# Raw weights and the conditioning matrix in 2 KB pieces through two rings, column sums and value weights a step apart, unread products at the norms

## The chip, the cores and the metric

The kernel runs on one core of a Trainium2 chip. The metric is the device time of one execution in microseconds (us); the kernel is built with Tile, a layer that puts every instruction into its engine's queue by a priority (the order of the program text, unless it is shifted) and adds the semaphores. The engines are TensorE (PE, with its weight loads PEld), VectorE (DVE), ScalarE (ACT), GpSimd (POOL) and SyncE (SP), which here does nothing but issue transfers. Each engine takes its own queue in order.

## The reference

One decoder layer on 512 tokens of width 2048, all in float32. Cut to what matters:

```
mod = silu(c) @ w_mod + b_mod                  # conditioning matrix: 2048 x 12288
sh1, sc1, g1, sh2, sc2, g2 = split(mod, 6)
h = rms_norm(x, norm_attn) * (1 + sc1) + sh1
qa, ka, va, qb, ckv, qi, ki, wi = split(h @ w_in)
out_a = sliding_window_attention(qa, ka, va, sinks, bias)     # 16 heads, window 128
out_b = sparse_attention(qb, rms_norm(ckv), w_uk, w_uv,       # 16 heads, 128 keys a query,
                         qi, ki, wi, bias)                    # chosen by the indexer's scores
x = x + g1 * (concat(out_a, out_b) @ w_out)
h = rms_norm(x, norm_ffn) * (1 + sc2) + sh2
u, g = split(h @ w_up)                                        # 2 x 5632 columns
x = x + g2 * ((silu(causal_conv3(u)) * g) @ w_down)
return rms_norm(x, norm_final)
```

## The kernel before

**Products.** Activations lie with their features on the partitions. A float32 product is made of three matmuls: weights and activations are each split into a rounded part and the rest (ACT casts, DVE subtracts), and `mm3` adds high by high, high by low and low by high.

**Slots.** The work of the big products is a list of *slots*. One slot is a quarter of a unit (128 output columns): 512 columns of raw weights, four `mm3`, so twelve matmuls. `drive` (L305) walks through the list. For slot i it asks for the raw weights up to `AHEAD_LOAD` slots ahead, for their split up to `AHEAD_SPLIT` = 3 slots ahead, gives PE the slot's matmuls, and then takes one `step()`: every running generator is advanced to its next `yield`. These generators are the rest of the work: the attention of a pair of heads (`pair_gen`), the keys and values of the next pair (`prep_gen`, L810), the convolution, and, last in each step, the conditioning matrix (`mod_gen`, L203).

**Raw weights.** `load_raw` (L120) loads one whole unit, 1 MB with 8 KB in each partition, into the ring `raw` of three buffers. Its four slots split their quarters from it (L128, L129), and the buffer comes free after the last. The same ring holds the indexer's weights (`fetch_qi`) and, in the attention stage and early in the gated MLP, the conditioning matrix (`ring_mod`).

**The conditioning matrix** is 24 groups of 512 columns, each of 16 row tiles. A group's row tiles come as four 1 MB pieces, one piece ahead of use. DVE multiplies a row tile by its 128 values of silu(c) and adds it to `macc` (`mod_acc`, L172 for the first, L174 for the others); then `mod_cols` sums over the partitions with eight small matmuls on PE (L184), and DVE adds the bias into `mod` (L219). Groups 0 to 7 are made at the start (most of them by PE, `mod_rows`), 8 to 13 in the stage of the sparse heads, three row tiles a step, 14 to 19 beside the output projection from two 1 MB buffers of their own, 20 to 23 early in the gated MLP.

**Stages in order of time.** First norm and indexer (0 to 200 us); sliding-window heads and the choice of keys (to about 372); sparse heads (to about 600); output projection `wo` (620 to 790); second norm `rs2`; gated MLP and its down projection (to 2100); the last quarter and the last norm.

**A norm** (`rstd_of`, L137): PE sums squares over the partitions (L142), ACT takes the root (L145), DVE inverts it and spreads it onto four diagonals (L146, L148), PE multiplies ones by these (L151), so that the result lies on all partitions. At rs2 the squares come from `wo_after` (L884): DVE adds the last product (L887), ACT squares, DVE adds (L878). DVE and ACT then make `h2h` and `h2l` for the first matmuls of the gated MLP (L155, L157, L1237).

Of the kernel before, what the change touches and what calls it, by code (L numbers as in the profile page):

```python
# [8 lines left out]
F32 = mybir.dt.float32  # L9
# [17 lines left out]
KEYW = 4 * P + 80  # L27
AHEAD_LOAD = 6
AHEAD_SPLIT = 3
# [3 lines left out]
def hybrid_trunk(ctx, tc, xT, cT, wm, bm, nrm, wik, wiq, wi1, sinks, kvn, wuk, wuv, rel, onehot,  # L33
# [85 lines left out]

    def load_raw(src, n, name):  # L120
        t = ring.tile([P, 2048], F32, tag="raw", bufs=3, name=name)
        sp.dma_start(t[:, :n], src)
        return t
# [12 lines left out]

    def rstd_of(accs, n, name, get, diag, nb=NB):  # L137

        ps = get(f"{name}s")
        for b in range(nb):  # L140
            for i, a in enumerate(accs):
                pe.matmul(ps[:, b:b + 1], a[:, P * b:P * b + P], ones[:, 0:1],  # L142
                          start=i == 0, stop=i == len(accs) - 1)
        r = const.tile([P, NB], F32, tag="rms", bufs=1, name=f"{name}r")
        act.activation(r[:, 0:nb], ps[:, 0:nb], AF.Sqrt, bias=epsc, scale=1.0 / n)  # L145
        dve.reciprocal(r[:, 0:nb], r[:, 0:nb])  # L146
        for b in range(nb):
            dve.tensor_scalar(diag[:, P * b:P * b + P], ident, r[:, b:b + 1], None, OP.mult)  # L148
        out = get(name)
        for b in range(nb):  # L150
            pe.matmul(out[:, P * b:P * b + P], ones, diag[:, P * b:P * b + P], start=True, stop=True)  # L151
        return out
# [49 lines left out]

    def mod_gen(groups, load, mp, get, per):  # L203
        pieces = [(g, q) for g in groups for q in range(4)]
        t = load(*pieces[0])
        n = 0
        for i, (g, q) in enumerate(pieces):
            nxt = load(*pieces[i + 1]) if i + 1 < len(pieces) else None
            if q == 0:
                acc = mod_accs(g, mp, 1)  # L210
            for k in range(4):
                mod_acc(acc, t[:, k], 4 * q + k)
                n += 1
                if n % per == 0:
                    yield
            if q == 3:
                ps = get(f"mps{g}")
                mod_cols(ps, acc)
                dve.tensor_tensor(mod[:, g], ps[:, 0:4], bm_sb[:, g], OP.add)  # L219
            t = nxt  # L220

# [29 lines left out]
    class Raw:  # L251
        def __init__(self, src, name):
            self.src, self.name, self.t = src, name, None

        def load(self):
            if self.t is None:
                self.t = load_raw(self.src.rearrange("p a b -> p (a b)"), 2048, self.name)

    class Slot:
# [3 lines left out]
        def load(self):  # L263
            self.raw.load()

        def split(self):
            if self.w is None:
                self.raw.load()
                self.w = split(self.raw.t, 512 * self.part, 512, f"{self.raw.name}_{self.part}")

    class Kept:
# [4 lines left out]
        def split(self):  # L276
            if self.w is None:
                n, part = self.part
                self.w = env["h2h"][:, n], env["h2l"][:, n]
                if self.raw:  # L280
                    self.raw.load()
                    split_to(*self.w, self.raw.t[:, 512 * part:512 * part + 512])

        def load(self):
            if self.raw:
                self.raw.load()

# [36 lines left out]
    with tc.tile_pool(name="ph0", bufs=1) as p0:  # L324
# [13 lines left out]
        def fetch_qi(j):  # L338
            fetched["q", j] = load_raw(wiq[j].rearrange("p a b -> p (a b)"), 2048, f"wiq{j}")

        maccs, mrows = {}, {}
        by_pe = [[0,1,2,3],[0,1,2,3]]+[[3],[2,3]]*3
# [72 lines left out]
        def cols0(j):  # L415
            accs = list(maccs.get(j, []))
            if j in mrows:
                if accs:
                    dve.tensor_tensor(accs[0], mrows[j], accs[0], OP.add)
                else:  # L420
                    accs = mod_accs(j, p0, 2)
                    act.copy(accs[0], mrows[j])
            cps[j] = bank("acc", f"mps{j}", (P, 4))
            mod_cols(cps[j], accs)

# [29 lines left out]
        def qi0(j, todo):  # L455
            for i in range(8):
                if i % 2 == 0:
                    w = split(fetched["q", j], 256 * i, 512, f"wiq{j}_{i}")
                ps = bank("tp", f"qip{j}_{i}")
# [17 lines left out]
        fetch(1)  # L477
        fill(16)
        cols0(0)
        post0(0)  # L480
        lo0(0)
        FK, FQ, CO, PO, LO = (4, 2, 4, 4, 5)
# [327 lines left out]
    def prep_gen(i):  # L810
        wr = p1.tile([P, 2 * P], F32, tag="wuk", bufs=1, name=f"wukr{i}")
        sp.dma_start(wr, wuk[i].rearrange("p a b -> p (a b)"))
        yield
        wh, wl = split(wr, 0, 2 * P, f"wuk{i}")
# [11 lines left out]
        if i % 2:  # L826
            return
        wr = tmp_t(f"wuvr{i}")
        sp.dma_start(wr, wuv[i // 2].rearrange("p a b -> p (a b)"))
        wh, wl = [t.rearrange("p (a b) -> p a b", a=2) for t in split(wr, 0, 512, f"wuv{i}")]  # L830
        v = p1.tile([P, NB, 2 * P], F32, tag="v", bufs=2, name=f"vb{i}")
# [48 lines left out]
    def norm_rows(name):  # L880
        rs = env["px"].tile([P, T], F32, tag="rs", bufs=1, name=name)
        return rstd_of([env["sacc"]], D, f"{name}ps", w_ps, rs)

    def wo_after(dt):  # L884
        def f(ps):
            xk = env["x2"][dt // 4][:, dt % 4]
            dve.scalar_tensor_tensor(xk, ps, mcol(2, dt), xk, OP.mult, OP.add)  # L887
            squares(dt, "sq2_")
        return f
# [283 lines left out]

    def ring_mod(g, q):
        t = load_raw(wm[g, q].rearrange("p a b -> p (a b)"), 2048, f"mraw{g}_{q}")
        return t.rearrange("p (a b) -> p a b", a=4)

# [5 lines left out]
    while idle:  # L1183
        step()
    start(mod_gen(range(8, 14), ring_mod, p1, sc_ps, 3), low=True)
    drive(slots, marks["qb0"], marks["wo"])
# [27 lines left out]
    sp.dma_start(env["x2"][0], xT[0])  # L1214
    px_mod = lambda g, q: mod_load(g, q, px, 2)
    start(mod_gen(range(14, 20), px_mod, px, o_bank, 3), low=True)
    at = marks["wo"] + 6
# [7 lines left out]

    rs_ps = norm_rows("rs2")
    for dt in range(0, KT, 4):
        dve.scalar_tensor_tensor(a2[:, dt:dt + 4], mod[:, 16 + dt // 4], 1.0, nrm_sb[:, 1, dt:dt + 4],
                                 OP.add, OP.mult)
    env["h2h"] = big.tile([P, KT, T], F32R, tag="b2", name="h2h")  # L1230
    env["h2l"] = big.tile([P, KT, T], F32R, tag="b3", name="h2l")
    for i in range(4):
        for kt in range(4 * i, 4 * i + 4):
            if kt % 4 == 0:
                xn2 = px.tile([P, 4, T], F32, tag="mraw", bufs=2, name=f"xn2_{i}")
            xk = xn2[:, kt % 4]
            dve.tensor_tensor(xk, env["x2"][kt // 4][:, kt % 4], rs_ps, OP.mult)  # L1237
            modulate(env["h2h"][:, kt], env["h2l"][:, kt], xk, a2[:, kt:kt + 1], mcol(3, kt))
# [5 lines left out]
    env["pd"] = pdc.__enter__()  # L1244
    start(mod_gen(range(20, 24), ring_mod, p2, o_bank, 2), low=True)
    drive(slots, marks["ff"] + 12, marks["join"])
# [96 lines left out]
```

## Time and profile before

| | |
|---|---|
| median of 3 runs | 2217.42 us (2216.13 to 2218.31) |
| profiled execution: its time | 2216.12 us |
| profiled execution: its span, first to last instruction | 2214.3 us |
| PE busy / DVE / ACT / POOL | 97% / 71% / 44% / 6% of the span |
| mean granted clock of PE | 0.986 |
| moved by DMA | 367 MB, 166 GB/s over the span |

A granted clock of 1.00 is 2.4 GHz, one of 0.50 is 1.2 GHz, and a mean in between is a share of time at each. PE's busy share is made of modelled ends of pipelined matmuls. So the stages matter more than the share over the whole span: where PE stands still, or runs at the lower clock, and what released it.

### The profile page before, as it was taken

How to read it: one execution, taken by the hardware profiler on the slowest of the kernel's cores; microseconds unless marked ns; L12 is line 12 of the kernel's file. 1: busy time of each engine (PE TensorE's matmuls, PEld its weight loads, DVE VectorE, ACT ScalarE, POOL GpSimd, SP SyncE). 2: the span in 40 equal slices, each digit the busy share in tenths (PEclk: the TensorE clock that was granted, in tenths of full speed). 3: DMA queues.
4: the chain of work that ended last, by engine and by line, in shares of the span. 5: the costliest groups of instructions: out<-in, count | busy, mean ns of one | idle time of the engine just before them, and what ended most of it. 6: DMA issues, size and time to landing. Idle time of an engine off the chain costs nothing.

```text
span 2214.3 us, 28348 instructions
## 1 busy us (share of the span) xinstructions
PE 2146.1 (97%) x10316; PEld 1743.9 (79%) x10316; DVE 1568.9 (71%) x2829; ACT 975.5 (44%) x1850; POOL 139.4 (6%) x184
## 2 busy tenths in 40 slices
PE   7999999988899999999999999999999999999997
PEld 4777876767788878888888888888888888888887
DVE  2887899766668769975757676665857666675766
ACT  4334977556642263333333343334333343334332
POOL 0000000000000000000101010110201010110200
PEclk9999999999899999999999999999999999999998
DMA  9771221655478827743736455553726455563662
GB/s 391 263 299 65 67 77 56 222 181 184 150 280 316 287 104 267 284 153 116 170 99 161 121 132 136 147 138 114 169 93 163 115 136 143 142 144 111 119 237 77
DMA packets 96524, 366.95 MB, mean 166 GB/s; under 512 B 10751, under 2 KB 17935, under 8 KB 65152
## 3 DMA queue, kind: packets, MB, share of 16 engines
q1 hardware_dynamic: 73184, 321.12, 41.6%
q0 software_dynamic: 22336, 42.45, 12.0%
q8 instruction: 81, 1.33, 0.2%
q10 hardware_dynamic: 864, 1.57, 0.2%
q14 instruction: 59, 0.48, 0.1%
HBM read 312.93 MB, written 52.17 MB: 165 GB/s over the span
## 4 chain that ended last, share of the span: by engine, by line
PE 82%; DVE 7%; DMA 6%; ACT 4%; issue 1%; SPq 0%; DVEq 0%; ACTq 0%
PE p L1034 6%; PE p L1033 6%; PE p L1032 6%; DMA mraw<-in_wm_dram 3%; DVE macc L174 1%; PE qip L133 1%; PE qip L134 1%; PE qip L135 1%; DMA ct<-cd 1%; PE mps L184 1%; PE o L745 1%; PE mrow L179 1%; DVE top L604 1%; DVE wk L607 1%; PE tpb L731 1%
## 5 line engine op out<-in xcount | busy, mean ns | idle before, releaser
L160 ACT CAST dh<-rq 128x512 fp32r<-128x512 f32 x240 | 149.1, 623 | 173.9 <-PE p L1034 151.1
L174 DVE SCALAR_TENSOR_TENSOR macc<-mraw,cact,macc 128x512 f32<-128x512 f32 x240 | 179.5, 748 | 31.7 <-DMA mraw<-in_wm_dram 28.3
L161 DVE TENSOR_TENSOR dl<-rq,dh 128x512 fp32r<-128x512 f32 x240 | 161.0, 685 | 37.3 <-ACT dh L160 36.5
L1034 PE MATMUL p<-dh,al 128*128 128x512 f32 x480 | 186.7, 389 | 0.0
L1032 PE MATMUL p<-dh,ah 128*128 128x512 f32 x480 | 186.7, 389 | 0.0
L1033 PE MATMUL p<-dl,ah 128*128 128x512 f32 x480 | 186.7, 389 | 0.0
L1043 POOL DMA_DIRECT2D cd<-co x72 | 61.5, 854 | 874.9 <-DVE co L1056 873.7
L1033 PEld LDWEIGHTS p<-dl,ah 128*128 128x128 f32 x480 | 90.2, 188 | 18.8
L1034 PEld LDWEIGHTS p<-dh,al 128*128 128x128 f32 x480 | 90.1, 188 | 18.6
L1032 PEld LDWEIGHTS p<-dh,ah 128*128 128x128 f32 x480 | 90.0, 188 | 18.7
L1059 DVE TENSOR_TENSOR v<-p,v 128x512 f32<-128x512 f32 x120 | 82.1, 685 | 6.3 <-PE p L1034 5.5
L1043 POOL DMA_DIRECT2D cd<-v x72 | 61.5, 861 | 128.0 <-DVE v L1061 73.1
L160 ACT CAST ah<-cu 128x256 fp32r<-128x256 f32 (+2 forms) x60 | 41.5, 692 | 50.2 <-DVE cu L958 29.0
L161 DVE TENSOR_TENSOR al<-cu,ah 128x256 fp32r<-128x256 f32 (+2 forms) x60 | 46.7, 779 | 22.9 <-ACT ah L160 20.4
L1056 DVE TENSOR_TENSOR co<-p,v 128x512 f32<-128x512 f32 x80 | 54.9, 686 | 8.0 <-PE p L1034 7.9
L978 DVE TENSOR_TENSOR rq<-rq,rq 128x512 f32<-128x512 f32 x80 | 52.2, 683 | 0.0
L466 DVE TENSOR_TENSOR qi<-qi,qip 128x512 f32<-128x512 f32 x56 | 38.3, 684 | 14.4 <-PE qip L135 13.7
L1045 POOL DMA_DIRECT2D cd<-co x8 | 4.4, 548 | 658.3 <-DVE co L1056 658.3
L711 ACT ACTIVATE sb<-sb,nmb 128x512 f32<-128x512 f32 (+2 forms) x64 | 35.4, 555 | 17.3 <-DVE nmb L709 16.9
L161 DVE TENSOR_TENSOR dl_t<-tw,dh_t 128x512 fp32r<-128x512 f32 x40 | 27.6, 692 | 21.5 <-ACT dh_t L160 21.5
L366 DVE SCALAR_TENSOR_TENSOR macc<-mraw,cact,macc 128x512 f32<-128x512 f32 x54 | 40.3, 746 | 0.4
L731 PE MATMUL tpb<-identr,sb 128*128 128x128 f32 x160 | 27.5, 296 | 12.4 <-DVE kb L549 6.3
(4486 smaller groups left out, 6393.9 us busy)
## 6 DMA issues: line engine op xcount, KB each, us to landing
mraw<-in_wm_dram SPq DMA_DIRECT2D x96, 1024.0 KB
rq<-in_wdn_dram SPq DMA_DIRECT2D x160, 256.0 KB
cd<-co POOLq DMA_DIRECT2D x80, 256.0 KB, 5.2
cd<-v POOLq DMA_DIRECT2D x80, 256.0 KB, 5.5
wiq<-in_wiq_dram SPq DMA_DIRECT2D x8, 1024.0 KB
wik<-in_wik_dram SPq DMA_DIRECT2D x8, 592.0 KB
xn<-in_xT_dram SPq DMA_DIRECT2D x4, 1024.0 KB
tbb<-biasd SPq DMA_DIRECT2D x16, 256.0 KB
```

Source lines behind the costliest of these rows:

```text
L160: act.copy(hi_t, full)
L161: dve.tensor_tensor(lo_t, full, hi_t.bitcast(F32), OP.subtract)
L174: dve.scalar_tensor_tensor(acc, t, cact[:, kt:kt + 1], acc, OP.mult, OP.add)
L366: dve.scalar_tensor_tensor(acc, fetched[j, q][:, kt % 4], cact[:, kt:kt + 1], acc, OP.mult, OP.add)
L731: pe.transpose(tp[:, i], self.s[:, c:c + P], ident)
L978: dve.tensor_tensor(self.b[out], self.b[a], self.b[b], OP.add)
L1032: pe.matmul(ps[b], ah[:, tok], wh, start=k == 0, stop=False)
L1033: pe.matmul(ps[b], ah[:, tok], wl, start=False, stop=False)
L1034: pe.matmul(ps[b], al[:, tok], wh, start=False, stop=k == 1)
L1043: pool.dma_start(cd[tb][dq], t, accum_op=OP.add)
L1056: dve.tensor_tensor(t, ps, box["v" if i == 1 else "u", b], OP.subtract)
L1059: dve.tensor_tensor(box["v", b], ps, box["v", b], OP.add)
```

## The change

Raw weights of a slot are loaded by themselves: 256 KB, 2 KB in each partition. The ring of three 8 KB buffers becomes two rings of 2 KB buffers in the same room: `raw` with seven (slots) and `mrw` with five (conditioning matrix; the indexer's weights alternate between the two). The conditioning matrix comes by row tile, four ahead in `mrw`, or seven ahead in eight buffers beside the output projection. In the stage of the sparse heads a step takes four row tiles in place of three, and the bias is added a step after the column sums. The value weights `wuv` are asked for together with `wuk`, and are split a step before their products. At the first norm and at rs2, PE gets matmuls (`keep_busy`) whose result nobody reads. The last unit of the output projection gets a priority that is 60 earlier for what follows its matmuls.

```
-AHEAD_LOAD = 6
+AHEAD_LOAD = 5
+RING = {"raw": 7, "mrw": 5}
...
-    def load_raw(src, n, name):
-        t = ring.tile([P, 2048], F32, tag="raw", bufs=3, name=name)
-        sp.dma_start(t[:, :n], src)
+    def load_raw(src, name, tag="raw"):
+        t = ring.tile([P, 512], F32, tag=tag, bufs=RING[tag], name=name)
+        sp.dma_start(t, src)
         return t
...
+    def keep_busy(n, name, src):
+        ps = bank("o", name)
+        for i in range(n):
+            pe.matmul(ps[:, :P], ones, src[:, :P], start=True, stop=True)
+
-    def rstd_of(accs, n, name, get, diag, nb=NB):
+    def rstd_of(accs, n, name, get, diag, nb=NB, busy=0):
...
                           start=i == 0, stop=i == len(accs) - 1)
+        if busy:
+            keep_busy(busy, f"{name}b", accs[0])
...
-    def mod_gen(groups, load, mp, get, per):
-        pieces = [(g, q) for g in groups for q in range(4)]
-        t = load(*pieces[0])
+    def mod_gen(groups, load, depth, mp, get, per):
+        pieces = [(g, kt) for g in groups for kt in range(KT)]
+        tiles = [load(*x) for x in pieces[:depth - 1]]
         n = 0
-        for i, (g, q) in enumerate(pieces):
-            nxt = load(*pieces[i + 1]) if i + 1 < len(pieces) else None
-            if q == 0:
+        for i, (g, kt) in enumerate(pieces):
+            if i + depth - 1 < len(pieces):
+                tiles.append(load(*pieces[i + depth - 1]))
+            if kt == 0:
                 acc = mod_accs(g, mp, 1)
-            for k in range(4):
-                mod_acc(acc, t[:, k], 4 * q + k)
-                n += 1
-                if n % per == 0:
-                    yield
-            if q == 3:
+            mod_acc(acc, tiles.pop(0), kt)
+            n += 1
+            if n % per == 0:
+                yield
+            if kt == KT - 1:
                 ps = get(f"mps{g}")
                 mod_cols(ps, acc)
+                yield
                 dve.tensor_tensor(mod[:, g], ps[:, 0:4], bm_sb[:, g], OP.add)
-            t = nxt
...
-        def load(self):
-            if self.t is None:
-                self.t = load_raw(self.src.rearrange("p a b -> p (a b)"), 2048, self.name)
+        def load(self, part):
+            if part not in self.t:
+                self.t[part] = load_raw(self.src[:, 512 * part:512 * part + 512], f"{self.name}_{part}")
...
+            for i in range(4):
+                fetched["q", j, i] = load_raw(src[:, 512 * i:512 * i + 512], f"wiq{j}_{i}", "mrw" if i % 2 else "raw")
...
-        fill(16)
+        fill(12)
+        keep_busy(2, "busy0", fetched[0, 2][:, 3])
+        fill(4)
+        keep_busy(2, "busy1", fetched[0, 3][:, 3])
         cols0(0)
         post0(0)
+        keep_busy(5, "busy2", maccs0[0])
         lo0(0)
...
         sp.dma_start(wr, wuk[i].rearrange("p a b -> p (a b)"))
+        if i % 2 == 0:
+            wv = tmp_t(f"wuvr{i}")
+            sp.dma_start(wv, wuv[i // 2].rearrange("p a b -> p (a b)"))
         yield
...
-        wr = tmp_t(f"wuvr{i}")
-        sp.dma_start(wr, wuv[i // 2].rearrange("p a b -> p (a b)"))
-        wh, wl = [t.rearrange("p (a b) -> p a b", a=2) for t in split(wr, 0, 512, f"wuv{i}")]
+        wh, wl = [t.rearrange("p (a b) -> p a b", a=2) for t in split(wv, 0, 512, f"wuv{i}")]
+        yield
...
-        return rstd_of([env["sacc"]], D, f"{name}ps", w_ps, rs)
+        keep_busy(9, f"{name}a", env["x2"][3][:, 2])
+        return rstd_of([env["sacc"]], D, f"{name}ps", w_ps, rs, busy=3)
...
-            dve.scalar_tensor_tensor(xk, ps, mcol(2, dt), xk, OP.mult, OP.add)
-            squares(dt, "sq2_")
+            with later(-60 if dt == KT - 1 else 0):
+                dve.scalar_tensor_tensor(xk, ps, mcol(2, dt), xk, OP.mult, OP.add)
+                squares(dt, "sq2_")
...
-    start(mod_gen(range(8, 14), ring_mod, p1, sc_ps, 3), low=True)
+    start(mod_gen(range(8, 14), ring_mod, 5, p1, sc_ps, 4), low=True)
...
-    px_mod = lambda g, q: mod_load(g, q, px, 2)
-    start(mod_gen(range(14, 20), px_mod, px, o_bank, 3), low=True)
+    start(mod_gen(range(14, 20), px_mod, 8, px, o_bank, 3), low=True)
...
     rs_ps = norm_rows("rs2")
+    keep_busy(9, "rs2c", env["sacc"])
...
-    start(mod_gen(range(20, 24), ring_mod, p2, o_bank, 2), low=True)
+    start(mod_gen(range(20, 24), ring_mod, 5, p2, o_bank, 2), low=True)
```

`px_mod` now loads one row tile into one of eight 2 KB buffers, and `xn2` at rs2 takes its tiles one by one from the same buffers.

## Rows read from the trace of the kernel before

**Rows 1.** Windows: length, busy PE, PEld, DVE, ACT, POOL; clock, DMA share, GB/s.

```profile
380.00:600.00 220.00, 190.30 (x1095) 151.09 (x1094) 154.95 (x330) 138.67 (x325) 0.00 (x0) 0.92 0.58 189
...
485.00:530.00 45.00, 44.38 (x287) 35.91 (x285) 35.45 (x80) 34.17 (x82) 0.00 (x0) 1.00 0.65 203
...
620.00:790.00 170.00, 169.07 (x795) 139.04 (x794) 125.59 (x195) 47.01 (x78) 0.00 (x0) 1.00 0.77 283
...
1000.00:2000.00 1000.00, 1000.00 (x4414) 828.02 (x4413) 658.51 (x1039) 384.16 (x624) 109.31 (x128) 1.00 0.53 135
```

**Rows 2.** Waits, 365 to 625 us: waiter, releaser: total us, times, longest.

```profile
DVE macc L174 <- DMA mraw<-in_wm_dram: 26.6, 6, 7.0
...
PE tpb L731 <- DVE kb L549: 6.3, 1, 6.3
PE tpb L731 <- ACT etb L732: 5.7, 4, 2.7
...
PE kbp L135 <- DVE wuk3l L129: 4.9, 1, 4.9
...
DVE mod L219 <- PE mps L184: 4.3, 3, 2.1
...
ACT qb4r_0h L128 <- DMA qb4r<-in_wi_dram: 3.4, 1, 3.4
...
PE kbp L133 <- ACT wuk7h L128: 3.0, 1, 3.0
...
PE kbp L133 <- ACT wuk1h L128: 2.3, 1, 2.3
```

**Rows 3.** Chain that ended last, 518 to 600 us: start, us, what.

```profile
525.41 12.33 DMA mraw<-in_wm_dram
537.84 0.75 DVE macc L174
...
539.33 0.71 DVE kb L549
540.08 1.11 PE tpb L731 x4
```

**Rows 4.** Waits of SP's queue, 365 to 625 us.

```profile
SPq L122 <- DVE macc L174: 47.8, 17, 6.4
...
SPq L122 <- DMA mraw<-in_wm_dram: 23.5, 5, 6.5
```

**Rows 5.** Chain that ended last, 2120 to 2135 us: a 256 KB load.

```profile
2126.21 4.27 DMA ct<-cd
```

**Rows 6.** Tile mraw, 365 to 625 us: its issues (ns minimum, median, maximum).

```profile
L122 SPq DMA_DIRECT2D mraw<-in_wm_dram x23: 327/328/358, 380.3 to 574.6; - x23
```

**Rows 7.** Windows with 2 KB pieces (rq, then ct) in flight.

```profile
1411.00:1418.00 7.00, 7.00 (x33) 5.79 (x32) 3.97 (x6) 2.49 (x4) 0.64 (x1) 1.00 0.91 211
...
2112.00:2124.00 12.00, 11.21 (x60) 8.96 (x59) 5.14 (x9) 2.39 (x4) 0.00 (x0) 1.00 1.03 393
```

**Rows 8.** Windows after the first norm and after rs2.

```profile
28.00:34.00 6.00, 5.94 (x13) 4.20 (x14) 3.03 (x6) 3.56 (x6) 0.55 (x1) 0.50 1.01 423
...
796.00:802.00 6.00, 4.30 (x9) 2.98 (x10) 5.99 (x11) 5.66 (x9) 0.00 (x0) 0.50 0.00 0
```

**Rows 9.** Timeline of PE, first norm: start, us, instruction, [idle before <-releaser].

```profile
19.74 1.13 PE L151 MATMUL rs1ps<-qi,ones 128*128 128x128 f32 x8 [0.25 <-DVE qi L148]
...
23.78 1.07 PE L179 MATMUL mrow<-mraw,cpad 128*32 128x512 f32 x8 [0.21 <-DMA mraw<-in_wm_dram]
...
27.90 1.22 PE L133 MATMUL ckv<-h1h,wik_0h 128*128 128x512 f32 x2 [1.29 <-ACT h1h L436]
...
30.03 0.79 PE L134 MATMUL ckv<-h1l,wik_0h 128*128 128x512 f32 x1
```

**Rows 10.** Timeline of PE at rs2.

```profile
792.48 1.05 PE L142 MATMUL rs2pssps<-ones,sq_acc 128*128 128x1 f32 x8 [2.23 <-DVE sq_acc L878]
794.42 1.16 PE L151 MATMUL rs2psps<-rs,ones 128*128 128x128 f32 x8 [0.89 <-DVE rs L148]
797.20 0.79 PE L133 MATMUL u0ps<-h2h,u0r_0h 128*128 128x512 f32 x1 [1.63 <-ACT h2h L155]
...
799.35 0.79 PE L134 MATMUL u0ps<-h2l,u0r_0h 128*128 128x512 f32 x1 [0.50 <-DVE h2l L157]
```

More of the change, by code (lines that the diff above doesn't have):

```diff
@@ L252, in __init__ @@
         def __init__(self, src, name):
-            self.src, self.name, self.t = src, name, None
-        def load(self):
-            if self.t is None:
-                self.t = load_raw(self.src.rearrange("p a b -> p (a b)"), 2048, self.name)
+            self.src, self.name, self.t = src.rearrange("p a b -> p (a b)"), name, {}
+        def load(self, part):
+            if part not in self.t:
+                self.t[part] = load_raw(self.src[:, 512 * part:512 * part + 512], f"{self.name}_{part}")
     class Slot:
@@ L263, in load @@
         def load(self):
-            self.raw.load()
+            self.raw.load(self.part)
         def split(self):
             if self.w is None:
-                self.raw.load()
-                self.w = split(self.raw.t, 512 * self.part, 512, f"{self.raw.name}_{self.part}")
+                self.load()
+                self.w = split(self.raw.t[self.part], 0, 512, f"{self.raw.name}_{self.part}")
     class Kept:
@@ L280, in split @@
                 if self.raw:
-                    self.raw.load()
-                    split_to(*self.w, self.raw.t[:, 512 * part:512 * part + 512])
+                    self.load()
+                    split_to(*self.w, self.raw.t[part])
         def load(self):
             if self.raw:
-                self.raw.load()
+                self.raw.load(self.part[1])
     def unit_slots(src, name, ps_of, acts, after):
@@ L338, in fetch_qi @@
         def fetch_qi(j):
-            fetched["q", j] = load_raw(wiq[j].rearrange("p a b -> p (a b)"), 2048, f"wiq{j}")
-        maccs, mrows = {}, {}
+            src = wiq[j].rearrange("p a b -> p (a b)")
+            for i in range(4):
+                fetched["q", j, i] = load_raw(src[:, 512 * i:512 * i + 512], f"wiq{j}_{i}", "mrw" if i % 2 else "raw")
+        maccs, mrows, maccs0 = {}, {}, []
         by_pe = [[0,1,2,3],[0,1,2,3]]+[[3],[2,3]]*3
@@ L423, in cols0 @@
             cps[j] = bank("acc", f"mps{j}", (P, 4))
+            maccs0[:] = accs
             mod_cols(cps[j], accs)
@@ L457, in qi0 @@
                 if i % 2 == 0:
-                    w = split(fetched["q", j], 256 * i, 512, f"wiq{j}_{i}")
+                    w = split(fetched["q", j, i // 2], 0, 512, f"wiq{j}_{i}")
                 ps = bank("tp", f"qip{j}_{i}")
@@ L1171, in hybrid_trunk, with ring_mod @@
             slots += last_slots(dq, half)
-    def ring_mod(g, q):
-        t = load_raw(wm[g, q].rearrange("p a b -> p (a b)"), 2048, f"mraw{g}_{q}")
-        return t.rearrange("p (a b) -> p a b", a=4)
+    def ring_mod(g, kt):
+        return load_raw(wm[g, kt // 4][:, kt % 4], f"mraw{g}_{kt}", "mrw")
     start(ahead(index_gen(), 0))
@@ L1214, in hybrid_trunk, with px_mod @@
     sp.dma_start(env["x2"][0], xT[0])
-    px_mod = lambda g, q: mod_load(g, q, px, 2)
-    start(mod_gen(range(14, 20), px_mod, px, o_bank, 3), low=True)
+    def px_mod(g, kt):
+        t = px.tile([P, 512], F32, tag="mraw", bufs=8, name=f"mraw{g}_{kt}")
+        sp.dma_start(t, wm[g, kt // 4][:, kt % 4])
+        return t
+    start(mod_gen(range(14, 20), px_mod, 8, px, o_bank, 3), low=True)
     at = marks["wo"] + 6
@@ L1233, in hybrid_trunk @@
         for kt in range(4 * i, 4 * i + 4):
-            if kt % 4 == 0:
-                xn2 = px.tile([P, 4, T], F32, tag="mraw", bufs=2, name=f"xn2_{i}")
-            xk = xn2[:, kt % 4]
+            xk = px.tile([P, T], F32, tag="mraw", bufs=8, name=f"xn2_{kt}")
             dve.tensor_tensor(xk, env["x2"][kt // 4][:, kt % 4], rs_ps, OP.mult)
```

## Prediction

> **What bounds the kernel now.** I read the windows first. From 1000 to 2000 us PE is busy 1000.00 of 1000 us at the full clock [rows 1]: the gated MLP is a solid row of matmuls, and earlier data can give nothing there. The output projection is nearly as full, 169.07 of 170 us. The stage of the sparse heads is not: from 380 to 600 us PE is busy 190.30 of 220 us, and the mean granted clock is 0.92. So 29.7 us are idle. The clock takes up to 8% of 220 us, 17.6 us; I count the part that falls on busy time, 17.6 x 190.3/220 = 15 us. Together 45 us lie in this stage, and no other stage has as much.
>
> Then the waits of that stage, to see what is late. DVE stands 26.6 us in six waits for a 1 MB piece of the conditioning matrix, and ACT 3.4 us for the first quarter of one weight unit, qb4r [rows 2]. Neither is PE, so I followed one to PE with the chain: the piece is issued at 525.41 us and lands 12.33 us later, the sum L174 runs at 537.84, behind it in DVE's queue come the keys kb, and at 540.08 PE gets its transposes, 6.3 us late [rows 2, 3]. Both engines take their queues in order, so whatever stands behind a late piece is late. PE's own long waits are of this kind: 6.3 (kb), 5.7 (etb), 4.9 (wuk3l), 3.0 (wuk7h) and 2.3 (wuk1h) us, 22.2 of the 29.7 us [rows 1, 2]. After such a gap the clock falls. Where no piece is late, from 485 to 530 us, PE is busy 44.38 of 45 us at clock 1.00 with the same work [rows 1]. So DVE (155 of 220 us) and ACT (139) are not the next bound close by.
>
> Last, SP's queue, to see why a piece is asked for late. Before L122, the line of the common ring, SP waits 47.8 us in 17 waits for sums that still read a buffer, and 23.5 us behind pieces under way [rows 4]. Three 1 MB buffers serve weights and matrix together: a weight buffer is held for four slots, so the matrix often has its next piece issued only when it is needed.
>
> **The change, part by part.**
>
> *Small pieces and two rings, sparse heads.* The lead in bytes stays at 1 MB (four row tiles), but a piece is needed and freed by row tile, and weights no longer wait for sums. How late will a piece be? The trace has one load of this size on a chain, 4.27 us from issue to landing among other transfers, against 12.33 us for the megabyte [rows 3, 5]: 1 - 4.27/12.33 = 65% of the lateness goes. The share of the stage's loss behind late pieces I take as 22.2/29.7 = 75%, for idle time and clock alike: 45 x 0.75 = 34 us. 34 x 0.65 = 22 us. Bounds: nothing (the same bytes per step, the same queues), and 38 us (all of the 34, and half of the rest). I take 22, as the clean 45 us show that PE keeps full when data are there.
>
> *SP.* Four issues replace one, each 0.33 us [rows 6]; at five pieces a step that is 1.6 us of a step of some 7 us (220 us over about 31 slots), hidden by the 71 us that SP waits now [rows 4]. If it did not hide, the bias tiles of the heads, which are queued behind, would land 1.3 us later, still ahead of their scores.
>
> *Four row tiles a step.* The total is unchanged; one more 0.75 us sum [rows 3] now stands in front of the next slot's splits, which are three slots ahead. Nothing, unless that lead is gone: then 0.75 us a step, 22 us over 30 steps. No row shows it; the clean stretch speaks against it.
>
> *Bias a step later, wuv a step earlier.* DVE's three waits for the column sums, 4.3 us, go [rows 2]. No wait of PE in that list is released by them, so nothing; at best 4 us, already within the 38. The load of wuv passes wuk in SP's queue and takes one of two temporary buffers for three steps longer; if the other were missing, one evacuation of a head's output would wait a step. Nothing, with that as the cost.
>
> *Output projection.* Its pieces lead by seven row tiles in place of one piece. PE loses 0.9 of 170 us there [rows 1], so the gain is at most 0.9. But sums that come early stand ahead of the weight splits on DVE (125.6 of 170 us busy); one stall like that of wuk3l would cost 5. I take nothing, between -0.9 and +5.
>
> *Gated MLP.* Its weights now lead by seven slots of buffers instead of a unit and more. PE is full [rows 1]; nothing, with a loss only if the transfers fail it (a rival).
>
> *Products at the first norm.* From 28 to 34 us PE is busy 5.94 of 6 us at clock 0.50 [rows 8]: work of 3 us at the full clock. Only what follows the wait for h1l at 30.03 sets the pace [rows 9], so about 4 us at half rate, worth 2.0. One product of this kind costs 1.13/4 = 0.28 us [rows 9]. busy0 (0.57) stands where PE waits 0.21 for the fourth quarter of the matrix: 0.36 late on the chain. busy1 fits behind the rows, and busy2 (1.4) into the 1.29 us before ckv. 2.0 - 0.4 = 1.6; as DMA runs at share 1.01 there and the next quarters come no sooner, I take 1.2 (bounds: 0.4 lost, 2 gained). That the clock stays up is assumed: PE would work where it has gaps now.
>
> *Products at rs2.* From 796 to 802 us PE is busy 4.30 us at 0.50 [rows 8], worth 2.15. The first nine products take 9 x 0.28 = 2.5 us of a gap of 2.23, the three fit into 0.89, the last nine take 2.5 of 1.63 [rows 10]: 0.3 and 0.9 late, but 0.5 of this is covered by the wait for h2l at 799.35. 2.15 - 0.3 - 0.4 = 1.4; I take 1.2 (bounds 1 lost, 2 gained). The earlier priority of the last unit can save one DVE instruction of 0.7 us in the 2.23 us; within the bounds.
>
> **Sum.** 2216.12 (profiled execution) - 22 - 1.2 - 1.2 = 2191.7 us. The median of the runs stands 1.3 above that execution: 2193.
>
> **Rivals.**
>
> *Half.* The next engine takes over: with pieces in time the heads wait for exponentials and copies in turn. For it: DVE and ACT are busy 70% and 63% of the stage, and 5.7 us of PE's waits end at a copy of ACT's. Against: the clean stretch. Half of the 22: 2193 + 11 = 2204.
>
> *All.* Nothing late is left, as the lead is by ring and no longer by chance: 38 in place of 22, so 2177.
>
> *It does nothing.* A piece of 256 KB waits in the same queue behind as many bytes. For it: 0.58 of DMA is used either way. The norms alone leave 2215; with 2 lost there, 2219.
>
> *Slower: small rows cost bandwidth.* Mechanism: 2 KB rows move slower than 8 KB rows, and the output projection, which moves 283 GB/s x 170 us = 48.1 MB [rows 1], becomes bound by transfers. Rows on both sides: 211 GB/s with 2 KB loads beside accumulating writes, 393 with 2 KB loads almost alone [rows 7]. At 211 the stage takes 228 us in place of 170: +58 - 24 = +34, 2250. It decides below 48.1 MB/(170 + 24) us = 248 GB/s. I take the 393, since the output projection has no accumulating writes. The Trainium skill (DMA: Bandwidth & Descriptors, Rules for kernel authors) speaks for this rival: it asks for at least 1 MiB per DMA for full bandwidth. Its table (section Bandwidth) has 138 GB/s at 64 KB and 341 at 1 MB; halfway, an estimate from that page, is 240, which would make the stage 200 us and the time 2223. By that rule the change is a loss; the trace's 393 GB/s with 256 KB loads does not agree with it.
>
> **How the numbers follow.** Forecast (2183 to 2200) 0.52; half 0.20; all 0.12; nothing 0.08; slower 0.08. No change is within 0.2%, 4.4 us, about what a measurement of this kernel can tell: below 2213 faster, 0.84; same 0.08; slower 0.08. The range takes in half and most of all: 2176 to 2213.
>
> **What would show it.** In the sparse heads: L174's waits for DMA below 9 us, SP's waits at L122 for sums gone, PE above 205 us of 220 in that work's length, clock near 1.00. From 28 to 34 us and in the 6 us after rs2, clock 1.00; if it is 0.50 still, the products bought nothing. The output projection keeps 170 us; if it grows and its DMA share is near 1, small rows cost. The prediction is wrong if DVE still waits for row tiles one after the other, or if PE waits for ACT and DVE without a late piece behind them.

## The result, and the profile after

The change makes the kernel about half a per cent slower: 2228.27 us median against 2216.45 on the same chip, a ratio of 1.0053 (95% interval 1.0034 to 1.0072). One of its six runs took 3062.74 us at a mean granted clock of 0.652; the ratio leaves it out, and the median of the other five is 2226.96. The prediction was 2193, and 2228 lies above its range of 2176 to 2213. The profiled execution took 2229.58 us, its span 2227.8.

First, where the 13.5 us between the two spans (2214.3 and 2227.8) were lost, by the first product of some tiles on PE:

| stage (first product to first product) | before, us | after, us | difference |
|---|---|---|---|
| start to the sparse heads (qb0) | 355.6 | 356.4 | +0.8 |
| sparse heads (qb0 to wo0) | 235.6 | 240.4 | +4.8 |
| output projection (wo0 to wo15) | 188.0 | 195.5 | +7.5 |
| last unit, norm rs2, eight MLP units (wo15 to u8) | 237.5 | 237.7 | +0.2 |
| the rest | 1197.6 | 1197.8 | +0.2 |

Each column is from one profile. The windows of the changed kernel, in the columns of [rows 1]:

```profile
380.00:600.00 220.00, 182.03 (x1074) 147.64 (x1074) 144.02 (x319) 137.90 (x330) 0.00 (x0) 0.91 0.56 170
485.00:530.00 45.00, 40.97 (x264) 34.19 (x265) 35.83 (x72) 29.81 (x69) 0.00 (x0) 0.92 0.67 202
620.00:790.00 170.00, 163.74 (x769) 133.56 (x768) 128.94 (x202) 49.09 (x88) 0.00 (x0) 0.99 0.86 296
1000.00:2000.00 1000.00, 1000.00 (x4414) 828.30 (x4413) 657.99 (x1040) 384.42 (x624) 109.11 (x128) 1.00 0.56 135
```

PE lost 8 us in the sparse heads, where the prediction had it gain, and 5 us in the output projection, which had been nearly full. The MLP is as before. The waits of the changed kernel, 365 to 625 us (L183 is the sum that was L174):

```profile
DVE macc L183 <- DMA mraw<-in_wm_dram: 36.8, 12, 6.0
...
PE tpb L748 <- ACT etb L749: 26.0, 6, 10.5
...
SPq L123 <- DMA mraw<-in_wm_dram: 25.0, 8, 5.6
...
SPq L123 <- DMA tbb<-biasd: 7.2, 3, 3.0
SPq L829 <- DMA tbb<-biasd: 6.3, 2, 3.2
```

DVE now waits longer for the pieces than in [rows 2], and twice as often. PE's 26.0 us end at ACT's copies etb. The last two lines are the odd ones: SP waits for a head's bias tile, tbb, before it issues loads that read no bias tile. The chain of the changed kernel, 389 to 474 us, shows the pieces themselves, and after the second of them how its delay reaches PE:

```profile
389.99 7.46 DMA mraw<-in_wm_dram
...
405.57 11.86 DMA mraw<-in_wm_dram
...
418.88 0.69 DVE kb L566
...
421.29 0.59 ACT etb L749
...
421.93 1.97 PE tpb L748 x8
...
431.46 9.72 DMA mraw<-in_wm_dram
...
442.06 8.40 DMA mraw<-in_wm_dram
...
473.28 9.48 DMA mraw<-in_wm_dram
```

The piece lands at 417.43, and the keys on DVE, then ACT's etb and PE's transposes follow in a row: PE's longest wait for etb, 10.5 us, is the late piece once more. On this chain a quarter of the bytes takes 7.46 to 11.86 us, nearly as long as the whole megabyte of [rows 3]. Over the whole stage, by the times at which loads raise their semaphores on landing (the semaphore records of the traces), the median from issue to landing is 7.75 us for 80 quarters, and 7.39 us for the 23 megabytes of the kernel before. What stands ahead of such a load is to be seen in the timeline of SP's queue:

```profile
404.90 0.51 SPq L703 DMA_DIRECT2D tbb<-biasd  x1
405.57 6.35 SPq L123 DMA_DIRECT2D mraw<-in_wm_dram  x4
```

and in the windows of 1 us at the end of that load (columns as in [rows 1]):

```profile
415.00:416.00 1.00, 0.00 (x0) 0.00 (x0) 0.00 (x0) 0.00 (x0) 0.00 (x0) 0.68 0.88 305
416.00:417.00 1.00, 0.00 (x0) 0.00 (x0) 0.00 (x0) 0.00 (x0) 0.00 (x0) 0.50 0.27 102
417.00:418.00 1.00, 0.00 (x0) 0.00 (x0) 0.48 (x1) 0.00 (x0) 0.00 (x0) 0.50 0.13 51
```

All compute engines stand, and at the end the share of the transfer engines is one eighth: 0.13 of sixteen is two. The kernel before has the same picture at the load of [rows 3], which was issued at 525.41; its queue and its windows:

```profile
522.84 0.51 SPq L686 DMA_DIRECT2D tbb<-biasd  x1
523.44 0.52 SPq L812 DMA_DIRECT2D wukr<-in_wuk_dram  x1
525.41 0.33 SPq L122 DMA_DIRECT2D mraw<-in_wm_dram  x1
...
535.00:536.00 1.00, 0.00 (x0) 0.00 (x0) 0.00 (x0) 0.00 (x0) 0.00 (x0) 1.00 0.30 123
536.00:537.00 1.00, 0.00 (x0) 0.00 (x0) 0.00 (x0) 0.00 (x0) 0.00 (x0) 0.58 0.12 49
537.00:538.00 1.00, 0.00 (x0) 0.00 (x0) 0.16 (x1) 0.00 (x0) 0.00 (x0) 0.50 0.14 57
```

Both kernels read a bias tile with `ap=[[1024 - 64, 2], [-1, 64], [1, n]]`: two halves of 64 rows. The Trainium skill (DMA: Bandwidth & Descriptors, Why a DMA increments its semaphore by 16 and not by 1) says that a transfer gets the largest number of engines, up to sixteen, that divides the outermost dimension on both sides; here that would be two, and the share of 0.13 agrees.

The traces' own records say it more directly. Between the first products of the sparse heads and of the output projection, exactly two packets are in flight for 44.0 of 235.6 us before and for 37.4 of 240.4 us after. And the tile issued at 404.90 us lands at 416.81, the piece issued behind it at 405.57 lands at 417.43, and the next five loads follow 0.6 us apart.

**Theory A**, then: a bias tile of 256 KB goes through two engines at some 50 GB/s, which is 256 KB / 50 = 5 us, 10 for the two heads of a pair. (This estimate is low: by the semaphore records a tile took 8.0 to 12.7 us from issue to landing before, and 7.7 to 13.7 after.) A load behind it in the queue has a part on these two engines, so it lands after them, whatever its own size. Its rivals: the pieces are issued late or with too little lead (B), and PE would wait for ACT and DVE anyway (C).

### The profile page after: what moved, and what is told of

It reads as the page before. It is cut to its first block, busy times and chain, and to the rows that moved or that the text cites. A ratio compares the mean times of both kernels' runs of the same rounds, so it can differ in the third digit from the quotient of the medians.

```text
span 2227.8 us, 30098 instructions
## 1 busy us (share of the span) xinstructions
PE 2149.5 (96%) x10376; PEld 1753.0 (79%) x10376; DVE 1568.6 (70%) x2829; ACT 976.2 (44%) x1850; POOL 139.1 (6%) x184
## 4 chain that ended last, share of the span: by engine, by line
PE 84%; DVE 6%; DMA 6%; ACT 3%; issue 1%; SPq 0%; DVEq 0%; ACTq 0%
PE p L1053 6%; PE p L1055 6%; PE p L1054 6%; DMA mraw<-in_wm_dram 4%; PE qip L134 1%; PE qip L135 1%; PE qip L136 1%; PE o L762 1%; PE tpb L748 1%; DVE macc L183 1%; PE mrow L188 1%; DVE wk L624 1%; DVE top L621 1%; PE mps L193 1%; DVE sa L726 1%
## 5 line engine op out<-in xcount | busy, mean ns | idle before, releaser
L183 DVE SCALAR_TENSOR_TENSOR macc<-mraw,cact,macc 128x512 f32<-128x512 f32 x240 | 179.7, 749 | 43.5 <-DMA mraw<-in_wm_dram 40.0
L748 PEld LDWEIGHTS tpb<-identr,sb 128*128 128x128 f32 x160 | 21.6, 161 | 33.7 <-ACT etb L749 29.6
```

What stands on the lines that cost most here:

```text
L183: dve.scalar_tensor_tensor(acc, t, cact[:, kt:kt + 1], acc, OP.mult, OP.add)
L748: pe.transpose(tp[:, i], self.s[:, c:c + P], ident)
```

## The experiments

All stages are those of the table above, from the profiled execution; ratios are to the kernel before on the same chip.

**e1 and e2, the bias tiles over sixteen engines**, in the changed kernel and in the kernel before. The table is stored in sixteen copies, so that the outermost dimension can be 16:

```diff
-    biasd = dram.tile([32, 2, 1024], F32, name="biasd")
+    biasd = dram.tile([32, 16, 1024], F32, name="biasd")
...
-        offset=biasd.offset + 2048 * (HEADS * g + head) + 384 * g + P - 1,
-        ap=[[1024 - 64, 2], [-1, 64], [1, n]])
+        offset=biasd.offset + 16384 * (HEADS * g + head) + 384 * g + P - 1,
+        ap=[[1024 - 8, 16], [-1, 8], [1, n]])
...
-                for k in range(2):
-                    pool.dma_start(biasd[:, k, T * i:T * i + T], t[:32, 2 + i])
+                pool.dma_start(biasd[:, :, T * i:T * i + T],
+                               t[:32, 2 + i].unsqueeze(1).broadcast_to([32, 16, T]))
```

> The changed kernel, but the bias table is stored in sixteen copies and a head's bias tile is read with an outermost dimension of 16 in place of 2; same values, same queue, same order. Theory A (a 256 KB bias tile goes through two of the sixteen transfer engines at some 50 GB/s, and every load behind it in SP's queue waits for these two, whatever its own size): bias loads land in under 4 us, DVE's waits for matrix pieces in the sparse heads fall from 36.8 us to under 10, that stage (first qb0 product to first wo0 product) from 240 us to 215 to 228, the time from 2228 to 2200 to 2215. Theory B (the pieces are late because they are issued late, their lead in bytes is too short, or because at most eight loads are in flight): waits above 28 us, time 2222 to 2232. Theory C (pieces late, but PE waits for ACT and DVE anyway): waits of DVE fall, the stage stays above 235 us.

> The kernel before, with the bias tiles over sixteen engines as in e1 and nothing else. Theory A: the long loads of 11.8 to 12.6 us of the kernel before, each issued right behind a bias tile, land in 4 to 7 us; DVE's waits for 1 MB pieces fall from 26.6 us to under 10, the stage from 235.6 us to 210 to 225, the time from 2216 to 2190 to 2206. Theory B: the megabyte itself is late; waits above 20 us, time 2212 to 2219. Theory C: waits fall, time 2210 or more.

Measured: e1 2190.12 us, ratio 0.9861 (0.9848 to 0.9874); e2 2186.59 us, ratio 0.9845 (0.9833 to 0.9858). The sparse heads take 200.5 and 200.6 us, where they took 240.4 and 235.6. In e1, 340 to 600 us, DMA issues with KB each and median us to landing, then DVE's waits:

```profile
mraw<-in_wm_dram SPq DMA_DIRECT2D x103, 256.0 KB, 4.6
tbb<-biasd SPq DMA_DIRECT2D x16, 256.0 KB, 4.1
...
DVE macc L183 <- DMA mraw<-in_wm_dram: 7.5, 11, 2.0
```

The same of e2:

```profile
mraw<-in_wm_dram SPq DMA_DIRECT2D x26, 1024.0 KB, 5.0
tbb<-biasd SPq DMA_DIRECT2D x16, 256.0 KB, 3.7
...
DVE macc L174 <- DMA mraw<-in_wm_dram: 2.8, 3, 2.1
```

Theory A holds, with more than it had set, and B and C fall: with nothing but the bias read changed, 35 to 40 us of the stage go, and exactly two packets are in flight for 2.3 us of it in e1 and 2.6 in e2. PE's waits for etb fall from 26.0 to 4.3 us in e1. And a second thing: a piece of 256 KB lands in 4.6 us, one of 1 MB in 5.0. Without the two engines in front, the size of a piece makes 0.4 us, and the two kernels' sparse heads differ by 0.1.

**e3, the queue apart from the engines**: `pool.dma_start` in place of `sp.dma_start` for the bias tile, still two engines.

> The changed kernel with the bias tiles still on two engines, but issued from GpSimd's queue instead of SP's. Theory A in the form that the order in SP's queue is what delays (pieces stand behind the bias tile on the same ring): DVE's waits for matrix pieces fall from 36.8 to under 15 us and the time to 2203 to 2218. In the form that the two engines are the bottleneck for any load that also uses them, from whichever queue: waits stay above 25 us, time 2222 to 2232. Theory B: as the second.

Measured: 2204.35 us, ratio 0.9930 (0.9917 to 0.9942), the stage 210.6 us. The issues and DVE's wait:

```profile
mraw<-in_wm_dram SPq DMA_DIRECT2D x92, 256.0 KB, 5.1
tbb<-biasd POOLq DMA_DIRECT2D x16, 256.0 KB, 10.8
...
DVE macc L183 <- DMA mraw<-in_wm_dram: 16.0, 14, 3.2
```

A bias tile takes 10.8 us here, but the pieces pass it: 5.1. So most of the loss, 29.8 of the 39.9 us between the changed kernel and e1, left with the tile's place in SP's queue; DVE's wait is 1 us more than I had set for it. The edit moves more than the place: GpSimd's queue sends the tile in packets of some 500 bytes (9536 for 4.79 MB), and SP no longer waits for the tile's buffer. Which engines the tile used there no view shows.

**e10, a dose**: the kernel before with four copies and four engines, `ap=[[1024 - 32, 4], [-1, 32], [1, n]]`.

> The kernel before with the bias tiles over four engines in place of two (four copies of the table); with sixteen it took 2187 us. Theory A (the price is the time that a 256 KB bias tile holds its few engines): with four it holds them half as long, so half of the 33 us or somewhat more comes back: 2192 to 2204 us, DVE's waits for 1 MB pieces in the sparse heads between 8 and 20 us (26.6 with two engines, 2.8 with sixteen). Theory L (not the engines but something else about the two-part read, its start or its order, is what the sixteen copies changed): no gain with four, 2213 to 2221, or all of it, 2185 to 2190, whatever the load's duration.

Measured: 2192.76 us, ratio 0.9884 (0.9862 to 0.9905); the stage 207.5 us in its profile, which is the slowest of its five runs (2198.67 us); DVE's waits for pieces in L174 5.4 us. By the ratios 1.16% of 1.55% comes back, three quarters. Exactly four packets are now in flight for 14.6 us of the stage, exactly two for 3.9, and a tile lands after 5.1 to 8.5 us: the number of engines follows the outermost dimension, and theory L falls. The time is just inside theory A's bounds, the waits are below what I set: they go faster than in proportion. One reading, not tested, is that a piece that is asked for some us ahead hides the first part of a delay.

**e5, the output projection's matrix in 1 MB pieces again** (two buffers, as before).

> The changed kernel with the matrix in the output projection back in 1 MB pieces and two buffers, as before; all else as changed. Theory D (seven pieces of lead and x stand ahead of the weights wo4 in SP's queue, and 2 KB rows move about 10 per cent less per busy share, so PE gets wo4's quarters late): the stage from wo0 to wo15 goes from 195.5 us back to 188 to 190, its PE gaps near 650 to 667 us vanish, time 2219 to 2224. Theory E (the stage is long because of its start, the late heads before it, or the clock): 194 us or more, time 2226 to 2231.

Measured: 2230.28 us, ratio 1.0041 (1.0027 to 1.0055); the stage 197.8 us. Neither theory: wo0 to wo4 falls from 64.3 to 59.7 us, but wo4 to wo15 grows from 131.2 to 138.1, where DVE waits 9.9 us in seven waits for the megabytes and PE 5.5 us in four for the column sums. So the size of the pieces alone doesn't mend it, though the clock of 0.96 after wo4 has a part in this profile. (The expectation's 10 per cent less per busy share is 6 by the windows 620 to 790 us: 283 GB/s at 0.77 against 296 at 0.86.) What the changed kernel's stage looks like at its gap, first SP's queue, then waits from 625 to 668 us:

```profile
628.79 0.33 SPq L123 DMA_DIRECT2D wo4r<-in_wo_dram  x1
629.54 0.33 SPq L123 DMA_DIRECT2D mraw<-in_wm_dram  x1
629.97 0.37 SPq L1234 DMA_DIRECT2D x<-in_xT_dram  x1
630.40 11.30 SPq L1238 DMA_DIRECT2D mraw<-in_wm_dram  x10
641.79 0.38 SPq L1246 DMA_DIRECT2D x<-in_xT_dram  x1
642.64 2.90 SPq L1238 DMA_DIRECT2D mraw<-in_wm_dram  x3
645.63 0.59 SPq L1246 DMA_DIRECT2D x<-in_xT_dram  x1
646.32 11.66 SPq L1238 DMA_DIRECT2D mraw<-in_wm_dram  x10
658.03 0.42 SPq L1246 DMA_DIRECT2D x<-in_xT_dram  x1
658.54 0.38 SPq L123 DMA_DIRECT2D wo4r<-in_wo_dram  x1
...
PE wo4ps L134 <- ACT wo4r_1h L129: 3.4, 1, 3.4
...
PE mps L193 <- DVE macc L183: 2.8, 1, 2.8
```

The second quarter of wo4 is issued 29.75 us after the first, behind 24 pieces and four 1 MB transfers x. When weights came a unit at a time, all four quarters went with the first.

**e8, weights earlier**: e1 with the weights asked for nine slots ahead instead of five while the output projection runs.

```diff
     at = marks["wo"] + 6
+    AHEAD_LOAD[0] = 9
...
     drive(slots, at, marks["ff"])
+    AHEAD_LOAD[0] = 5
```

> The changed kernel with the bias tiles over sixteen engines (2190 us), and the weights of the output projection asked for nine slots ahead in place of five, so that three of wo4's quarters pass the last 4 KB-row transfer x and six matrix pieces in SP's queue. Theory H (the output projection lost 6.4 us, 193.2 against 186.8, because quarters by slot lead by five slots where a whole unit led by six to nine, and stand behind the burst of matrix pieces and x): the stage 186 to 189 us, time 2183 to 2187. Theory I (the burst of ten pieces and x takes the bandwidth, at 2 KB rows, whichever stands first): the stage 192 us or more, time 2188 to 2192.

Measured: 2186.17 us, ratio 0.9854 (0.9832 to 0.9875), the stage 189.7 us: 3.5 of the 6.4 us come back, in the time as theory H had it, in the stage 0.7 short of it. wo0 to wo4 stays at 63.6. The ratio alone doesn't tell e8 from e1 (0.9861, 0.9848 to 0.9874).

**e11, and a shorter burst**: e8 with the matrix three pieces ahead in place of seven (depth 4 for 8). The 190.2 us in the expectation should read 189.7.

> The changed kernel with bias tiles over sixteen engines and weights nine slots ahead (2186 us), and the matrix in the output projection three pieces ahead in place of seven, so that six pieces and not ten stand in SP's queue between the first two transfers x. Theory M (what is left of the output projection's loss, 190.2 against 186.8 us, is this burst: it delays x and the first wo4 quarters): the first wo0 to the first wo4 product goes from 63.6 us to 60 to 61, the stage to 187 to 188.5, time 2182 to 2185. Theory N (a shorter lead makes the sums wait for pieces, and PE for the column sums): the stage 191 us or more, time 2187 to 2192.

Measured: 2180.02 us, ratio 0.9825 (0.9807 to 0.9844); wo0 to wo4 59.5 us, the stage 185.4. Its windows from wo0 to wo4 and from there to wo15:

```profile
557.00:617.00 60.00, 58.28 (x331) 47.08 (x332) 51.49 (x92) 34.50 (x75) 0.00 (x0) 1.00 0.76 263
617.00:743.00 126.00, 125.81 (x578) 104.29 (x577) 98.91 (x158) 33.63 (x56) 0.00 (x0) 1.00 0.89 300
```

With the same 2 KB rows, PE is all but full and the stage is 2.6 us shorter than in the kernel before, 1.4 shorter than in e2. Theory M holds, with 2 us more than it had set: what was left was the burst that the lead of seven makes. This is the lowest median of all, but its interval overlaps those of e2 (0.9833 to 0.9858) and e7 below: that the small pieces, mended, beat 1 MB pieces is not shown.

**e12, these two edits alone**, the bias tiles still on two engines.

> The changed kernel, bias tiles still over two engines, with the two edits of the output projection alone (weights nine slots ahead, the matrix three pieces ahead). Theory M: the output projection is a loss of its own; its stage goes from 195.5 us to 187 to 189, the time from 2228 to 2219 to 2222, what is left over the kernel before being the sparse heads' 5 us less what FFN and norms gave. Theory O (the projection's loss came from the late sparse heads, whose loads stand in the same queue): the stage 192 us or more, time 2225 to 2230.

Measured: 2219.33 us, ratio 0.9992 (0.9981 to 1.0002); the stage 185.2 us, the sparse heads 239.3. The output projection was a loss of its own, and without it the change comes out level with the kernel before. One profile is a loose measure of this stage (e10, whose code there is that of the kernel before, has 192.6 us, with a clock of 0.97 after wo4), but e11, e12 and e13, with both edits, have 185.2 to 185.4, and the five profiles with 2 KB pieces and neither edit 191.7 to 195.5.

**e9, the early sums**: e1, with the sums of groups 8 to 13 held until the last indexer weights are split.

```diff
+    last = slots[marks["qb0"] - 1].w[0][:, :KT].bitcast(F32)
+    c2 = env["cact2"] = const.tile([P, KT], F32, name="cact2")
+    dve.scalar_tensor_tensor(c2, last, 0.0, cact, OP.mult, OP.add)
     start(mod_gen(range(8, 14), ring_mod, 5, p1, sc_ps, 4), low=True)
```

> The changed kernel with the bias tiles over sixteen engines (2190 us), and the sums of the matrix groups 8 to 13 held until the last indexer weights are split, by a copy of the factors that is made from them; their first pieces still load early. Theory J (sixteen sums of 0.75 us that run early, from 192 to 262 us, sit in a stage in which DVE sets the pace, and cost there the 2.6 us by which the sparse heads start late): the first product of the sparse heads at 355 to 356.5 us in place of 358.0, their stage 200 to 202 us as DVE has room there, time 2186.5 to 2189. Theory K (the sums cost nothing early, or cost as much later): start 357.5 or later, or the stage 203 us or more; time 2189 to 2193.

Measured: 2189.56 us, ratio 0.9873 (0.9851 to 0.9895). The sparse heads start at 355.5 us, 2.5 earlier than in e1, and take 206.4, 5.9 more. The time does not move, as theory K had it: the sums that the small pieces let run early cost as much where they had stood. (The 2.5 us are no firm figure; in the changed kernel, e8, e11 and e12, which are alike up to there but for the bias read, the start lies between 356.4 and 359.6. Counted from the first indexer product, which the norm before it moves, the stretch takes 314.9 to 315.2 us in the four kernels with 1 MB pieces, 315.0 in e9, and 317.6 to 320.7 in the nine with early sums: theory J's price is real, 2.4 to 5.8 us, and is paid again in the sparse heads.)

**e4, e7 and e13, the products that nobody reads.** e4 is the changed kernel without them and without the earlier priority, e7 is e2 with both, e13 is e11 without the products.

> The changed kernel without the products that nobody reads at the two norms and without the earlier priority at the last unit of the output projection; small pieces, rings and steps stay. Theory F (the products are worth what the prediction had, 1.2 us at each norm): 2230 to 2232. Theory G (the first norm's gain is lost again before the sparse heads and the products at the second norm cost as much as they hold up the clock; from the last unit to the first MLP product it took 19.5 us with them against 18.0 before): 2225 to 2228, that stretch 18 us, the clock at the two norms 0.50 for some us again.

> The kernel before with the bias tiles over sixteen engines (2187 us) and the products at the two norms with the earlier priority; 1 MB pieces and one ring as before. Theory F: 2183 to 2185, the first matmul of the sparse heads 1 to 1.6 us earlier, 355.4 to 354. Theory G: 2186 to 2189; the stretch from the last unit to the first MLP product goes from 19.0 to 19.5 us or more.

> The fastest version so far (the changed kernel with bias tiles over sixteen engines, weights nine slots ahead, the matrix three pieces ahead: 2180.0 us, its five runs within 2.2 us) without the products that nobody reads; the earlier priority at the last unit stays. Theory F (the products are worth the 1.2 us at each norm that the prediction had): 2181.5 to 2184 us. Theory G (they hold the granted clock up, but PE then waits for the same data): 2178 to 2181 us; the first indexer product starts at 38.8 to 39.2 us as with them, and the time from the last unit's first product to the ninth MLP unit's (237.7 us with them) changes by under 0.5 us, with the clock at 0.50 in more of the windows.

Measured: e4 2232.08 us, ratio 1.0058 (1.0037 to 1.0079), against the change's 1.0053; e7 2182.44, ratio 0.9841 (0.9820 to 0.9862), against e2's 0.9845; e13 2186.66, ratio 0.9870 (0.9851 to 0.9889), against e11's 0.9825. Two pairs show no difference, the third shows 0.45% for the products, more than either theory. At their own places they do little. The windows 28 to 34 us of the changed kernel, e4 and e7 in this order (columns of [rows 1]), each from its own profile:

```profile
28.00:34.00 6.00, 5.00 (x26) 2.74 (x24) 4.14 (x8) 4.04 (x7) 0.55 (x1) 1.00 1.02 426
```

```profile
28.00:34.00 6.00, 5.94 (x22) 3.48 (x22) 3.76 (x7) 3.65 (x6) 0.55 (x1) 0.73 1.01 425
```

```profile
28.00:34.00 6.00, 4.98 (x29) 3.95 (x29) 4.36 (x9) 4.80 (x9) 0.55 (x1) 1.00 1.02 426
```

From 28 to 34 us the products hold the clock at 1.00 in both, against the 0.50 of [rows 8] and 0.73 without them. But they don't always keep it from falling: of the nine profiles with them, six have 1.00 from 19 to 34 us, and three (e3, e7, e9) have 0.72 from 19 to 25 us instead. The first indexer product follows the clock, not the size of the pieces. It comes at 38.7 to 38.9 us in those six and at 40.4 to 40.5 in those three; without the products at 40.4 and 40.5 where the clock was 0.50 from 28 to 34 us (before, e2), and at 39.0 to 39.2 where it was 0.72 or 0.73 (e4, e13, and e10 with its 1 MB pieces). So the products are worth between nothing and 1.8 us there. What let the clock rise sooner in e4 than in [rows 8] no run tells.

From wo15 to u8 it is 236.1 to 239.0 us in the eight profiles with 2 KB pieces and the products, and 238.3 and 238.1 in e4 and e13 without: too near to tell a gain. (With 1 MB pieces it is 238.4 with them, in e7, and 237.5 to 242.3 without.) Theory G's point that they lengthen the way from the last unit to the first MLP product holds with 1 MB pieces and not with small ones: it is 19.5 or 19.6 us in all nine profiles with them; without, 18.0 to 19.0 in the three with 1 MB pieces, and 19.9 in e4 and e13. Of the 3.5 us between the spans of e11 and e13, 3.7 lie in the sparse heads, where no such product stands and where the clock of e13 is 0.97 from 500 to 556 us. The profile of e13 is the fastest of its runs, 3.1 us below their median, so it shows only a part of the 0.45%. What makes that difference is open.

## Why the prediction failed, step by step

**What bounds the stage: right.** I put 34 us of the sparse heads' loss down to late pieces. With the bias read mended and nothing else, that stage of the kernel before gives back 35.0 us (235.6 to 200.6). That the two numbers lie so close is partly luck: the 34 was a share of PE's waits, taken over other bounds (380 to 600 us).

**The step that failed: "1 - 4.27/12.33 = 65% of the lateness goes".** It took the 12.33 us for the price of a megabyte. They were the price of the bias tile in front: pieces of 256 KB took 7.46 to 11.86 us in the same place, and with that tile over sixteen engines the megabyte takes 5.0. It was also the second longest of the 23 megabytes of the stage, not a typical one. The comparison of [rows 3] with [rows 5] put two loads side by side that differed in size and in what stood ahead of them in the queue, and I gave it all to the size. The 22 us of the forecast were then a loss of 4.8. (The upper bound has a slip of its own: "all of the 34, and half of the rest" is 39.5, not 38; nothing hangs on it.)

**Why a loss and not nothing.** SP's issues, counted as 0.33 us and hidden, were not: SP waits 25.0 + 7.2 + 6.3 = 38.5 us at loads of the ring and of wuk for pieces and bias tiles under way (23.5 in [rows 4]), and 3.5 us in e1. The records show two things that held it. The five buffers of `mrw` were full: the load of 410.80 us goes out 0.87 us after the piece in its buffer lands, which had been issued at 401.35. And the loads take eight semaphores in turn (1072 of 1076 have that of the eighth load before), so a load waits while the eighth before it is under way: the one of 440.80 goes out 0.06 us after the tile issued at 430.86 lands. What each is worth, and how much is due to the larger number of loads that can stand behind a tile, no run separates. It belongs to the two engines in any case, as the stages of e1 and e2 are level. And the loss is a loose figure: the four profiles of the changed kernel with two engines (itself, e4, e5, e12) have 237.2 to 240.4 us, against one profile before. SP's waits for sums, which were to be gone, were 42.0 us in 63 waits from 365 to 625 us, after 47.8 in 17.

**Output projection: 0, bounded by -0.9 and +5; measured +7.5.** The bound was made from DVE's stalls. What came was SP's queue: quarters of weights asked for singly, behind 24 pieces and four x. e8, e11 and e12 show it; e12 makes both edits at once, and e8 and e11 take them one after the other.

**The rival "slower" had the side and the place right, the mechanism wrong.** The stage moved 296 GB/s from 620 to 790 us, above the 248 from which it decides, and with 2 KB rows it becomes shorter than before in e11. The rule of the Trainium skill cited there (DMA: Bandwidth & Descriptors, Rules for kernel authors: at least 1 MiB per DMA) gave the right sign, but not the cause: in e11 the pieces are still 256 KB, and in e1 they land in 4.6 us. The page's table, from which the 240 GB/s were estimated, is for loads that GpSimd issues; here SP issues them.

**The norms, 1.2 us each.** "That the clock stays up is assumed", the prediction says. At the first norm it did in six of nine profiles; there the first indexer product comes 1.5 to 1.7 us earlier than the 40.4 of the kernel before, about what was forecast, and in the other three no earlier. The changed kernel's gain of 1.6 us is then lost before the sparse heads to a term that the sum did not have: the early sums, 317.6 us from the first indexer product to qb0 against 315.2 before. At rs2 the clock still falls in this profile, for a shorter time; the window of the changed kernel that answers to 796 to 802 us in [rows 8]:

```profile
811.00:817.00 6.00, 4.75 (x19) 3.49 (x19) 5.99 (x11) 6.00 (x9) 0.00 (x0) 0.81 0.00 0
```

In the first 5 us of the MLP it is 1.00 in four of the nine profiles with the products, 0.66 to 0.79 in the others, and 0.50 in all five without. By u8 no gain can be told: 237.7 us from wo15, 237.5 before, in the spread given above.

**Four row tiles a step, bias a step later, wuv earlier, MLP: nothing.** The MLP agrees; the others were not tried apart.

## What to carry to other kernels

When a load takes long, look at what stands ahead of it in its queue and at the share of the transfer engines in the last us before it lands. Here a share near 2 of 16 with everything idle was one narrow transfer, and a quarter of the size did not mend the load that waited behind it. An outermost dimension of 16 in the narrow access pattern did (e2), one of 4 did three quarters of it (e10), and another queue most of it (e3). Whoever cuts transfers smaller also sets their order anew: weights that set the pace must be asked for ahead of the bursts that do not.

## What the runs showed that was not expected

The dose is not linear: two, four and sixteen engines for the same 256 KB tile gave DVE waits of 26.6, 5.4 and 2.8 us in the kernel before and ratios of 1, 0.9884 and 0.9845. And 2 KB rows cost PE nothing in e11 with many loads in flight, though they cost the transfer engines something: from wo4 to wo15 they move 300 GB/s at a share of 0.89, where the kernel before moves 297 at 0.81. A piece takes 4.6 us from issue to landing in e1, a megabyte 5.0 in e2.
